# The first modulation weights and the residual rows are loaded ahead of the constants' second part and the long filters' tables

## The chip, the core and the metric

The kernel runs on one core of one Trainium2 chip. The metric is the time of one execution on the device in microseconds (us). The core's engines work side by side, each through its own instructions in order: PE (matrix multiplication), DVE (vector), ACT (scalar and table functions), POOL (general purpose) and SP (which here only issues DMA transfers). ACT and POOL issue transfers too.

## The reference, cut to what matters

The kernel computes two layers of a token trunk over 256 context tokens and 256 latent tokens (512 rows of 1024 numbers, float32). Every layer modulates and normalises the rows, projects them into three mixers (a long convolution called Hyena, a gated delta rule called GDN, and attention), merges these and goes through a mixture of experts. The change touches the first layer's start, of which this is the part:

```python
def hyena_filters(L, lp):                       # depends on weights alone, not on x
    ...
    z = jnp.concatenate([t, jnp.cos(f * w), -jnp.sin(f * w)], axis=-1)
    hdn = jnp.sin(freq * (z @ lp['hy_f_w1'] + lp['hy_f_b1']))
    hdn = jnp.sin(freq * (hdn @ lp['hy_f_w2'] + lp['hy_f_b2']))
    h = hdn @ lp['hy_f_w3']
    window = jnp.exp(-t * jnp.abs(lp['hy_decay'])) + HY_MOD_SHIFT
    return h * window                           # goes through an rfft before its use

def gdn_features(qkv, a, b, lp):
    qkv = jax.nn.silu(centred_conv(qkv, lp['gdn_conv_w']))
    ...
    g = -jnp.exp(lp['gdn_a_log']) * jax.nn.softplus(a + lp['gdn_dt_bias'])
    beta = jax.nn.sigmoid(b)

# each layer: shift, scale and gate are silu(c) @ w_ada + b_ada;
# h = rms_norm(x) * (1 + scale) + shift; then one input projection p = h @ w_in,
# whose columns are cut into hyena, q, k, v, a, b, the rotary key and the rest
```

## The kernel before, in words

The kernel is one long program that a planner writes at build time. Every instruction goes through a helper (`Lane.call`, line 210), so that all of them carry line 210 in the profile; they are told apart by their tiles. The planner keeps an estimated clock for each engine and decides from it which ready piece of work is written next. On the chip each engine then runs its list strictly in order.

The pieces are of two kinds. **Items** form the main line: each has some loads (`loads`) and work behind them (`post`). `enqueue` puts the loads of items in a queue, and `pump` issues them, each into a page (`pg`, 256 or 512 KB) of on-chip memory; `pump(force=n)` issues n of them at once. **Streams** are generators (`start`, `step`) that run beside the main line: after each `yield` the planner fits the stream's next part between items.

The first layer's start has these parts:

- `ada_items(0, 0)`: the first two of the layer's modulation vectors, as 16 tiles 128x1024 of `w_ada` (512 KB each) and two rows of `b_ada`, loaded on SP's queue. PE multiplies each tile by the condition `sc` (four matmuls 128x512 to a tile, in two loop steps of two). `ada_post` then copies the result from the accumulator (`bank`), turns it and makes `t_mod` and `t_A`, the shift and scale of each channel.
- `load_x`: four tiles of rows 128x1024 (x and ctx), loaded on ACT's queue. `norm_rows` squares and sums them on ACT and normalises them.
- `make_h`: 32 transposes on PE, and behind them eight pieces of h: scale and shift on DVE (128x256), a cast to the rounded type on ACT (the high part), and a subtraction on DVE or POOL (the low part). A product with such a pair takes three matmuls.
- `abkr`: the first projection block, for the gates a and b and the rotary key (24 matmuls 128x512). Its weights lie at tile `pg_28`. Behind it come the gates: `t_beta`, `t_gt`, `t_nal`, `t_gg`.
- `qkv(0)`: six projection blocks k0, k1, q0, q1, v0, v1 (24 matmuls each), each followed by a short convolution and silu on ACT and DVE. Eight transposes behind v1 stand at the end of this part.
- the stream `filters(0)`: the Hyena filters. Its loads (`dft` 512 KB, `hy_decay` 512 KB, `hy_f_w3` 256 KB on SP; six small ones on POOL) are issued when it is started. Then: Abs of `hy_decay`, a cast of `dft`, two Exp on ACT, two rounds of (matmul 64x256, six or seven DVE operations, Sin on ACT), four matmuls 64x512 with `w3` that give the filters, and after these 48 matmuls 128x512 with the table `dft`. The last part is held until `make_h` is written (`self.hold`, "first").
- `cst[1]`: the second part of the constants, 128x1468 (734 KB), one load on SP.
- the stream `vectors(0)` and `gains(0)`: small vectors, loaded by POOL.

What each engine does next at the start is set by three things: the order in which the loads stand on SP's queue, the planner's order of the streams' parts among the items, and on the chip the wait of each instruction for its inputs.

Of the kernel before, what the change touches and what calls it, by code (L numbers as in the profile page):

```python
# [111 lines left out]
CFIRST = COFF["ones"][0]  # L112
# [246 lines left out]
class Trunk:  # L359
# [1994 lines left out]
    def build(self):  # L2354
        nc, M, a = self.nc, self.M, self.a
# [2 lines left out]
        self.cond()  # L2358
        plan0 = self.ada_items(0, 0)
        items = self.layer(0)  # L2360
        nc.sync.dma_start(out=self.cst[1], in_=a["cst"][:, CFIRST:])
        self.start("filters", self.filters(0))
        self.gains(0)
        self.start("vectors", self.vectors(0))
        self.enqueue(plan0)
        xs = self.load_x(0)
        self.enqueue(items)
        self.pump(force=21)
        xn = []

        def norm():
# [196 lines left out]
```

## Time and profile before

| | |
|---|---|
| median of three runs | 2118.0 us (2116.41 to 2120.69) |
| the profiled execution's own time | 2112.58 us |
| its span in the trace | 2110.9 us |
| PE busy | 1853.4 us, 88% of the span |
| DVE busy | 1296.4 us, 61% |
| ACT busy | 855.6 us, 41% |
| POOL busy | 338.4 us, 16% |
| DMA moved | 402.67 MB, mean 191 GB/s |

All times of a trace count from the span's start and come from the one profiled execution. The granted clock (PEclk) is the share of full TensorE speed: 1.00 is 2.4 GHz and 0.50 is 1.2 GHz. A matmul that is written as fp32r runs on rounded operands. An idle time in brackets stands ahead of the instruction that ended it, with what that instruction waited for.

### The profile page before, as it was taken

What the parts mean: (1) busy time and instruction counts of PE and PEld (TensorE: products, weight loads), DVE (VectorE), ACT (ScalarE), POOL (GpSimd) and SP (SyncE); (2) the same over time, 40 slices, a digit from 0 to 9 for tenths busy, and PEclk for the clock granted to TensorE, in tenths of its full rate; (3) what the DMA queues carried; (4) which work ended last, traced back from release to release, by engine and by line L of the source; (5) the groups of instructions that cost most, each with busy time, mean ns of one, the idle gap of its engine ahead of it and who ended that gap; (6) DMA issues with size and microseconds to landing.
All of it is one profiled execution on the core that took longest, in us unless ns stands there. A gap on an engine that the chain in (4) does not pass through costs nothing. (4 is left out here: it accounts for less than half of the span.)

```text
span 2110.9 us, 32623 instructions
## 1 busy us (share of the span) xinstructions
PE 1853.4 (88%) x12413; PEld 1368.1 (65%) x12414; DVE 1296.4 (61%) x2775; ACT 855.6 (41%) x1477; POOL 338.4 (16%) x318
## 2 busy tenths in 40 slices
PE   5899989999999998699999289977999966899993
PEld 1776777777768776588888176966778855333330
DVE  2667666655576567899999567675777846111113
ACT  3342423344434423388887344523455421011101
POOL 1211221000123004311100211111012203100002
PEclk8999999999999999899999699988999986999996
DMA  9727111402362456699994839223324458699961
GB/s 332 249 82 214 56 40 52 124 21 81 120 180 59 120 189 248 230 373 384 378 383 177 276 137 291 67 43 94 80 80 132 132 174 333 225 394 390 383 239 69
DMA packets 295617, 402.67 MB, mean 191 GB/s; under 512 B 43941, under 2 KB 185771, under 8 KB 295449
## 3 DMA queue, kind: packets, MB, share of 16 engines
q1 hardware_dynamic: 271512, 360.38, 50.9%
q0 software_dynamic: 11040, 19.81, 2.8%
q10 hardware_dynamic: 12896, 20.28, 2.7%
q8 instruction: 100, 1.64, 0.3%
q14 instruction: 69, 0.56, 0.1%
HBM read 393.52 MB, written 23.20 MB: 197 GB/s over the span
## 5 line engine op out<-in xcount | busy, mean ns | idle before, releaser
L210 PE MATMUL bank<-pg,pg 128*128 128x512 f32 (+7 forms) x10732 | 1663.8, 390 | 77.0 <-ACT pg L210 48.0
L210 PEld LDWEIGHTS bank<-pg,pg 128*128 128x128 f32 (+5 forms) x10732 | 1212.9, 167 | 476.8 <-issue 199.2
L210 DVE TENSOR_TENSOR pg<-pg,pg 128x1024 fp32r<-128x1024 f32 (+14 forms) x697 | 603.2, 897 | 169.3 <-ACT pg L210 158.8
L210 ACT CAST pg<-pg 128x1024 fp32r<-128x1024 f32 (+3 forms) x460 | 427.9, 965 | 235.0 <-DVE pg L210 157.8
L210 ACT COPY pg<-bank 128x512 f32<-128x512 f32 (+5 forms) x414 | 171.0, 444 | 346.0 <-PE bank L210 301.7
L210 PE MATMUL bank<-cst,pg 128*128 128x128 f32 (+3 forms) x935 | 144.7, 292 | 103.8 <-DVE pg L210 49.7
L210 PEld LDWEIGHTS bank<-cst,pg 128*128 128x128 f32 (+1 forms) x935 | 117.8, 159 | 156.7 <-issue 54.1
L210 POOL TENSOR_TENSOR pg<-pg,pg 128x512 f32<-128x512 f32 (+3 forms) x77 | 131.6, 1714 | 446.2 <-DVE pg L210 274.1
L210 ACT ACTIVATE pg<-bank 128x512 f32<-128x512 f32 (+1 forms) x116 | 60.7, 534 | 197.2 <-PE bank L210 175.0
L210 DVE SCALAR_TENSOR_TENSOR pg<-bank,vec,pg 128x510 f32<-128x510 f32 (+3 forms) x112 | 73.5, 657 | 56.1 <-ACT pg L210 54.2
L210 DVE SCALAR_TENSOR_TENSOR pg<-pg,bank 128x512 f32<-128x512 f32 (+1 forms) x92 | 54.2, 601 | 84.6 <-ACT pg L210 72.3
L210 ACT ACTIVATE pg<-pg 128x512 f32<-128x512 f32 (+4 forms) x71 | 49.0, 698 | 138.7 <-DVE pg L210 123.4
L210 POOL DMA_INDIRECT yd<-pg,t_vi x28 | 29.0, 1037 | 467.6 <-ACT pg L210 232.0
L210 POOL TENSOR_TENSOR pg<-pg 128x512 f32<-128x512 f32 (+1 forms) x18 | 20.4, 1142 | 454.5 <-ACT pg L210 306.9
L210 DVE TENSOR_TENSOR pg<-bank,pg 128x512 fp32r<-128x512 f32 (+4 forms) x120 | 69.1, 596 | 30.7 <-ACT pg L210 23.5
L210 DVE COPY pg<-bank 128x512 f32<-128x512 f32 x24 | 16.6, 692 | 112.1 <-PE bank L210 90.8
L210 DVE TENSOR_TENSOR pg<-pg,bank 128x512 f32<-128x512 f32 (+1 forms) x44 | 27.0, 613 | 79.8 <-PE bank L210 77.0
L210 ACT CAST pg<-bank 128x512 fp32r<-128x512 f32 (+1 forms) x72 | 35.7, 517 | 96.9 <-PE bank L210 72.7
L210 ACT ACTIVATE pg<-bank,t_amx,t_asq 128x512 f32<-128x512 f32 (+1 forms) x48 | 33.9, 707 | 75.1 <-DVE t_amx L210 75.1
L210 ACT ACTIVATE pg<-bank,vec 128x512 f32<-128x512 f32 (+3 forms) x64 | 41.3, 646 | 53.6 <-PE bank L210 47.3
L210 PE MATMUL bank<-pg,sc 128*32 128x512 f32 x384 | 53.9, 634 | 0.7 <-DMA pg<-in_w_ada_dram 0.7
L210 DVE TENSOR_REDUCE pg<-pg 128x128 f32<-128x1024 f32 (+15 forms) x128 | 43.1, 336 | 4.4
(250 smaller groups left out, 785.0 us busy)
## 6 DMA issues: line engine op xcount, KB each, us to landing
pg<-in_moe_w_dram SPq DMA_DIRECT2D x384, 512.0 KB
pg<-in_w_in_dram SPq DMA_DIRECT2D x120, 512.0 KB
pg<-in_w_ada_dram SPq DMA_DIRECT2D x96, 512.0 KB
pg<-in_w_out_dram SPq DMA_DIRECT2D x24, 512.0 KB
pg<-modd ACTq DMA_DIRECT2D x12, 512.0 KB
pg<-yd SPq DMA_DIRECT2D x12, 512.0 KB
pg<-in_mla_w_uq_dram SPq DMA_DIRECT2D x16, 288.0 KB
pg<-gcd POOLq DMA_DIRECT2D x16, 256.0 KB, 3.8
```

The lines of the kernel that those rows point to most:

```text
L210: return f(*a, **k)
```

## The change

Two calls move behind the loads of the modulation weights, the small vectors and the rows of x: the load of `cst[1]` and the start of the stream `filters(0)`. `pump` is split: 18 loads (the 16 tiles of `w_ada` and the two rows) come first, and the three others (of the item abkr and the first block) behind. No arithmetic is added or removed.

```diff
--- before.py
+++ after.py
@@ -2358,14 +2358,15 @@
         self.cond()
         plan0 = self.ada_items(0, 0)
         items = self.layer(0)
-        nc.sync.dma_start(out=self.cst[1], in_=a["cst"][:, CFIRST:])
-        self.start("filters", self.filters(0))
         self.gains(0)
         self.start("vectors", self.vectors(0))
         self.enqueue(plan0)
         xs = self.load_x(0)
+        self.pump(force=18)
+        nc.sync.dma_start(out=self.cst[1], in_=a["cst"][:, CFIRST:])
+        self.start("filters", self.filters(0))
         self.enqueue(items)
-        self.pump(force=21)
+        self.pump(force=3)
         xn = []
 
         def norm():
```

The planner then orders the rest anew. The rows below are from the engines' instruction lists in program order; `x2` counts repeats, `<-` separates the output from the inputs, and the numbers behind a tile's name only tell tiles apart. First SP's queue, before, from its third transfer, and the end of the modulation loads:

```order
4 L210 DMA cst_72<-in_cst_dram 128x1468
5 L210 DMA pg_5_105<-in_dft_dram 128x1024
6 L210 DMA pg_4_104<-in_hy_decay_dram 128x1024
7 L210 DMA pg_3_103<-in_hy_f_w_dram 64x1024
8 L210 DMA pg_10_136<-in_w_ada_dram 128x1024
9 L210 DMA pg_11_138<-in_w_ada_dram 128x1024
...
25 L210 DMA pg_27_170<-in_w_ada_dram 128x1024
26 L210 DMA pg_28_172<-in_w_in_dram 128x8x16
```

And the same queue in the changed kernel:

```order
4 L210 DMA pg_7_120<-in_w_ada_dram 128x1024
5 L210 DMA pg_8_122<-in_w_ada_dram 128x1024
...
21 L210 DMA pg_24_154<-in_w_ada_dram 128x1024
22 L210 DMA cst_72<-in_cst_dram 128x1468
23 L210 DMA pg_27_162<-in_dft_dram 128x1024
24 L210 DMA pg_26_161<-in_hy_decay_dram 128x1024
25 L210 DMA pg_25_160<-in_hy_f_w_dram 64x1024
26 L210 DMA pg_28_172<-in_w_in_dram 128x8x16
```

The four transfers of `cst`, `dft`, `hy_decay` and `hy_f_w3` (2.06 MB) now stand between the modulation tiles and the weights of abkr, and the place of abkr in the queue is unchanged. On POOL's queue the filters' small transfers stand behind those of the vectors in the same manner.

Next ACT's list. Before, the filters' Abs, cast, two Exp and two Sin (the 64x256 rows) stand ahead of the squares of the rows of x (`t_rma`), and the cast of abkr's weights and of k0's weights (`pg_29`) stand far behind:

```order
10 L210 ACTIVATE pg_4_104<-pg_4_104 128x1024
11 L210 CAST pg_35_197<-pg_5_105 128x1024
12 L210 ACTIVATE pg_38_202<-pg_4_104,cst_72 128x1024
13 L210 ACTIVATE pg_39_204<-pg_4_104,cst_72 128x1024
14 L210 ACT_TABLE_LOAD
15 L210 ACTIVATE pg_37_201<-pg_37_201 64x256
16 L210 COPY vec_216<-bank_66 128x113
17 L210 ACTIVATE pg_37_201<-pg_37_201 64x256
18 L210 ACTIVATE pg_50_272,t_rma<-pg_6_128 128x1024
...
31 L210 CAST pg_69_357<-pg_28_172 128x1024
...
43 L210 CAST pg_88_492<-pg_29_176 128x1024
```

In the changed kernel, with what each row waits for behind it (`DVE_49` is DVE, `PE_49` is PE, `Pool_49` is POOL, `DMAHW...` a transfer; the first row is the last cast of h, and the Sin are the 64x256 rows):

```order
29 L210 CAST pg_68_376<-pg_63_339 128x512 [waits DVE_49]
30 L210 ACTIVATE pg_26_161<-pg_26_161 128x1024 [waits DMAHW5_49]
31 L210 CAST pg_70_386<-pg_27_162 128x1024 [waits DMAHW2_49]
...
34 L210 CAST pg_75_413<-pg_29_176 128x1024 [waits DMAHW1_49,PE_49]
35 L210 COPY pg_72_390<-bank_67 16x512 [waits DMAHW6_49,PE_49]
...
40 L210 ACT_TABLE_LOAD [waits DMAHW3_49,DMAHW4_49,DVE_49]
41 L210 ACTIVATE pg_2_102<-pg_2_102 64x256 [waits Pool_49]
42 L210 ACT_TABLE_LOAD
43 L210 ACTIVATE t_beta<-bank_69 128x32 [waits DVE_49]
...
47 L210 ACTIVATE pg_78_526<-pg_72_390 128x512 [waits DVE_49,Activation_49]
48 L210 ACT_TABLE_LOAD [waits DVE_49]
49 L210 ACTIVATE pg_2_102<-pg_2_102 64x256 [waits PE_49]
```

The filters' work on ACT has moved behind the casts of h. The two Sin now alternate with the gates (`t_beta`) and the short convolution of k0 (row 47). Rows 40 to 48 hold three table loads, where the kernel before had one ahead of both Sin and one ahead of `t_beta`. The loads of rows 40 and 48 carry the wait for DVE that is the wait for the argument of the Sin behind them; the one of row 42 waits for nothing.

Last PE's list. Before, the matmuls of the two sine rounds (rows 7 and 17) and the four filter matmuls (`pg_3`, the tile of `hy_f_w3`) lie among and right behind the modulation tiles (`sc`):

```order
7 L210 MATMUL bank_65<-pg_2_102,t_fw_99 64x256
...
17 L210 MATMUL bank_67<-pg_37_201,t_fw_100 64x256
...
21 L210 MATMUL bank_64<-pg_25_166,sc 32x512 x2
22 L210 MATMUL bank_68<-pg_3_103,pg_37_201 128x512
23 L210 MATMUL bank_69<-pg_3_103,pg_37_201 128x512
24 L210 MATMUL bank_64<-pg_26_168,sc 32x512 x2
...
27 L210 MATMUL bank_63<-pg_3_103,pg_37_201 128x512
28 L210 MATMUL bank_65<-pg_3_103,pg_37_201 128x512
```

In the changed kernel the same work stands behind abkr's 24 matmuls (which end at row 70): rows 71 and 89 are the sine rounds, 72 turns abkr's result, 73 to 88 are block k0, 90 works on the gates, 93 and 94 are filter matmuls, and 95 begins block k1:

```order
71 L210 MATMUL bank_68<-pg_2_102,t_fw_157 64x256
72 L210 MATMUL bank_69<-cst_71,pg_72_390 128x16 x4
73 L210 MATMUL bank_70<-pg_58_306,pg_75_413 128x512 x2
...
88 L210 MATMUL bank_70<-pg_68_376,pg_76_414 128x512
89 L210 MATMUL bank_63<-pg_2_102,t_fw_158 64x256
90 L210 MATMUL bank_65<-t_gg,cst_72 128x16 x2
...
92 L210 MATMUL bank_64<-cst_71,pg_77_423 128x113
93 L210 MATMUL bank_66<-pg_25_160,pg_2_102 128x512
94 L210 MATMUL bank_67<-pg_25_160,pg_2_102 128x512
95 L210 MATMUL bank_68<-pg_58_306,pg_81_545 128x512 x2
```

The 48 matmuls with `dft`, which stood right behind the transposes of h in the kernel before and surrounded abkr, follow in the changed kernel among the third and fourth blocks. From PE's list on behind the eight transposes after v1, both kernels have the same order.

## Rows read from the trace of the kernel before

**Rows 1.** Windows of 20 us: busy time by engine, granted clock, DMA share, GB/s.

```profile
40.00:60.00 20.00, 11.55 (x48) 8.62 (x49) 12.39 (x33) 6.98 (x11) 0.00 (x0) 0.66 1.15 323
...
80.00:100.00 20.00, 15.98 (x66) 12.63 (x65) 10.93 (x35) 7.00 (x12) 6.58 (x14) 0.91 0.81 257
...
120.00:140.00 20.00, 20.00 (x113) 15.60 (x112) 8.92 (x24) 8.52 (x14) 5.58 (x6) 1.00 0.09 27
...
160.00:180.00 20.00, 17.06 (x94) 13.48 (x93) 16.76 (x36) 4.27 (x8) 2.83 (x2) 0.91 0.63 203
```

**Rows 2.** DMA view of 35-36 us, of 37-38 us, and issues in the first 75.

```profile
DMA packets 114, 0.41 MB, mean 406 GB/s; under 512 B 15, under 2 KB 15, under 8 KB 114
...
DMA packets 1542, 0.17 MB, mean 165 GB/s; under 512 B 1540, under 2 KB 1540, under 8 KB 1542
...
cst<-in_cst_dram SPq DMA_DIRECT2D x1, 734.0 KB
```

**Rows 3.** Timeline 0-40 us: start, duration, engine, tile, count, idle time before.

```profile
10.51 1.06 ACT L210 ACTIVATE pg<-pg 128x1024 f32<-128x1024 f32 x1 [5.04 <-DMA pg<-in_hy_decay_dram]
...
12.40 2.18 ACT L210 ACTIVATE pg<-pg,cst 128x1024 f32<-128x1024 f32 x2
...
23.70 0.54 DVE L210 TENSOR_SCALAR pg<-bank,t_fv 64x256 f32<-64x256 f32 x1 [9.94 <-PE bank L210]
...
26.58 0.42 ACT L210 ACTIVATE pg<-pg 64x256 f32<-64x256 f32 x1 [10.69 <-DVE pg L210]
...
35.32 1.05 PE L210 MATMUL bank<-pg,sc 128*32 128x512 f32 x4 [0.24 <-DMA pg<-in_w_ada_dram]
...
36.30 1.98 PE L210 MATMUL bank<-pg,pg 64*128 64x512 f32 x4
```

**Rows 4.** Timeline 40-75 us.

```profile
46.69 0.58 ACT L210 COPY pg<-bank 128x512 f32<-128x512 f32 x1
...
49.45 0.38 DVE L210 SCALAR_TENSOR_TENSOR t_A<-t_mod,vec 128x4 f32<-128x4 f32 x4 [1.94 <-ACT t_mod L210]
...
55.76 1.05 ACT L210 CAST pg<-pg 128x1024 fp32r<-128x1024 f32 x1 [1.21 <-DVE pg L210]
...
56.84 1.22 DVE L210 TENSOR_TENSOR pg<-pg,pg 128x1024 fp32r<-128x1024 f32 x1 [1.16 <-ACT pg L210]
...
57.98 2.80 DVE L210 TENSOR_SCALAR pg<-bank,t_A,t_mod 128x256 f32<-128x256 f32 x6
...
60.70 0.68 DVE L210 TENSOR_TENSOR pg<-pg,pg 128x512 fp32r<-128x512 f32 x1
...
67.03 0.87 DVE L210 TENSOR_TENSOR pg<-pg,pg 128x512 fp32r<-128x512 f32 x1
```

**Rows 5.** Timeline 75-120 us.

```profile
78.02 0.57 ACT L210 COPY pg<-bank 16x512 f32<-16x512 f32 x1
...
79.46 0.87 DVE L210 TENSOR_TENSOR pg<-bank,cst 32x256 f32<-32x256 f32 x2
...
80.36 0.42 DVE L210 TENSOR_TENSOR pg<-pg,pg 32x256 f32<-32x256 f32 x1
...
86.45 1.28 ACT L210 ACT_TABLE_LOAD   x1 [4.67 <-DMA rb<-in_router_b_dram]
...
87.75 0.20 ACT L210 ACTIVATE t_beta<-bank 128x32 f32<-128x32 f32 x1
...
92.70 1.53 DVE L210 SCALAR_TENSOR_TENSOR pg<-bank,vec,pg 128x510 f32<-128x510 f32 x2
...
92.84 1.19 PE L210 MATMUL bank<-t_gg,cst 128*128 128x16 f32 x6 [3.96 <-DVE t_gg L210]
...
94.99 0.69 DVE L210 SCALAR_TENSOR_TENSOR pg<-pg,pg 128x512 f32<-128x512 f32 x1 [0.76 <-ACT pg L210]
...
100.99 16.53 PE L210 MATMUL bank<-pg,pg 128*128 128x512 f32 x70 [0.53 <-DVE pg L210]
...
117.36 1.03 PE L210 MATMUL bank<-cst,pg 128*128 128x128 f32 x8
```

## The prediction

> **What bounds the kernel now.** I read the windows first, then the timeline of the first 120 us engine by engine, then the transfers, and last the two kernels' instruction lists. Over the whole span PE is busy 88%, so PE's idle time is what can be lost or won. The windows show where it lies at the start: PE is busy 11.55 of 20 us from 40 us on, 15.98 of 20 from 80 us on, and without a gap from 120 to 140 us [rows 1]. The reader is to see two things in this. From about 118 us on PE is the bound, and what shifts its work there shifts the end. Ahead of that PE waits for ACT and DVE, and the one long wait of the blocks is 3.96 us for the gates (`t_gg`), at 88.9 us [rows 5].
>
> The landmark is the set of eight transposes behind block v1. It starts at 117.36 us [rows 5], and by then both kernels have done the same work on PE: modulation, h, abkr, six blocks, and all matmuls of the filters. Behind it PE's order is the same in both. So the forecast is the time at which the changed kernel comes to this point.
>
> **Step 1, the loads.** 734, 512, 512 and 256 KB, in sum 2.06 MB, leave the front of SP's queue. With large packets the queue moves 406 GB/s [rows 2], so the modulation tiles come 2.06 / 0.406 = 5.1 us earlier. Before, PE takes a tile at 35.32 us, two more follow at 1.29 us each (524 KB / 406 GB/s), so the last comes at 37.9 and now at 32.8; its matmuls take 1.05 us [rows 3] and end at 33.9. From the copy of the result (46.69) to the end of `t_A` (49.45 + 0.38) it takes 3.14 us [rows 4]: `t_A` stands at 37.0 and not at 49.8. That is 12.8 us won. The bounds are the full 5.1 us, and nothing if the rows of x share the rate for longer. What stands behind the four transfers, abkr's weights first, keeps its place and lands when it did (about 39.6, an estimate: at 37 to 38 us its small packets still come at 165 GB/s [rows 2]). Moving the small transfers on POOL's queue costs nothing: the filters now need them some 30 us later.
>
> **Step 2, what ACT and DVE do behind it.** Each runs in order, and the filters' work, which before lay in the time in which both waited for loads (10 to 36 us), now stands behind h. I add it up along both lists.
>
> - h starts at 37.0. Its first six DVE operations take 2.80 us and a low part 0.68 [rows 4]: about 40.4. Then DVE reorders abkr's weights (0.49, an estimate for four copies from the gap ahead of the cast): 40.9; ACT casts them, 1.05, and DVE subtracts, 1.22 [rows 4]: 43.2.
> - The rest of h: all of h takes DVE from 57.98 to 67.90 us [rows 4], 9.92, less the 3.48 done: 6.4, so 49.6.
> - The filters' Abs, cast and two Exp on ACT took from 10.51 to 14.58 [rows 3], 4.07: 53.7. The cast of k0's weights, 1.05: 54.8. The copy of abkr's result, 0.57: 55.4. On DVE k0's low part ends at 56.0, the rotary key takes 0.87 + 0.42 [rows 5], `t_tokv` an estimated 0.3: 57.6.
> - The first sine's argument takes DVE from 23.70 to 26.54 [rows 3], 2.84: 60.5. Its table load carries the wait for that argument: 1.28 [rows 5], then Sin, 0.42 [rows 3]: 62.2. The table load for the gates, 1.28: 63.5.
> - The gates, from `t_beta` at 87.75 to `t_gg`, ready when PE's wait ends at 92.84 (less 0.06): 5.03: 68.5. The convolution of k0 on DVE and its silu on ACT, from 92.70 to 95.68, 2.98 [rows 5]: 71.5.
> - The second sine's argument, 2.84: 74.3; its table load, which waits for it, and Sin, 1.70: 76.0.
>
> Only at 76.0 can PE start the four filter matmuls and block k1, which stands behind them in its list. Before, half of them ran at 36.3 us [rows 3]. In the meantime PE has only abkr and k0, some 11 us of work, and stands idle for most of 63 to 76 us. This is the new wait that takes the place of those for the modulation and the gates.
>
> **Step 3, from there to the landmark.** PE has the four filter matmuls (1.98 us for half of them [rows 3], 3.96), and of the 144 + 24 + 48 = 216 matmuls of blocks, abkr and filters all but the 48 of abkr and k0. 70 take 16.53 us [rows 5], so 168 take 39.7: 76.0 + 3.96 + 39.7 = 119.7. To that comes the clock. After the 3.96 us wait the window of 80 to 100 us has a mean grant of 0.91, 1.8 us less of full speed in 20; the window of 40 to 60 us, behind a longer idle time, has 0.66, and by PE's busy share of it (11.55 / 20) 3.9 us [rows 1]. I take 2.5, nearer the first, since from 76 us on PE has work without a gap: 122.2 us, against 117.36. The sum is **+4.8 us**.
>
> The bounds of the terms: the three table loads cost between nothing (if all run ahead of their operands) and 3.84, and I take 3.84 because two of them carry the wait; the loads' gain between 5.1 and nothing; the clock between 1.8 and 3.9. ACT also issues three small transfers ahead of the first sine. In the kernel before, ACT's table load waited 4.67 us behind the same three [rows 5]; here they stand behind loads that are long in by 57 us, so I take nothing, and at worst it is 57.3 + 4.67 - 60.5 = 1.5. That makes +1.0 to +12.0 with everything at one end, and +1.5 to +8 for what can fall together.
>
> On the table loads the trace gives 86.45 + 1.28 = 87.73 and the next ACTIVATE at 87.75 [rows 5]: 1.30 us from the load's start to the instruction behind it. The Trainium skill, "ScalarE: Activation LUTs", section "What ACT_TABLE_LOAD costs", says that a change of table costs about 1.28 us of load and 1.38 us of drain. This row shows the load and no drain. By the page the three loads would cost 3 x 1.38 = 4.1 us more, and the sum would be +8.9.
>
> **The rivals.**
>
> *The chain costs PE less, and the kernel is faster.* For it: `t_A` is 12.8 us earlier, and my sum lets ACT and DVE alternate. If they overlap, DVE alone sets the end: 9.9 of h, 0.5, three low parts (3.7), 1.7 of key and constants, 2 x 2.84, some 4.6 of gates and 2.2 of convolution are 28.3 us from 37.0, 65.3, and with the last table load and Sin 67.0. Then 67.0 + 43.7 + 1.8 = 112.5, 4.9 us faster: 2113. Against it: the lists show operands that go from one engine to the other at nearly every step. It decides if the second Sin ends before 71.2 (117.36 - 43.66 - 2.5).
>
> *A later wait takes it back.* For it: from 160 to 180 us PE is busy 17.06 of 20 us [rows 1]. If that wait ends with a load that does not move, 2.9 of the 4.8 us are lost in it: +1.9, 2120. Against it: PE is full for 40 us ahead of it, and ACT and DVE take their work from PE there.
>
> *The loads give less, or the table loads cost more.* If the rows of x on ACT's queue hold the rate, the modulation comes when it did, and the chain starts 5.1 us later: +9.9, 2128. If each of the three table loads holds ACT for twice its 1.28 us, it is 3.84 more: +8.6, 2127. The page named above speaks for this second half, since its drain is of that size. For the first half: the queue runs at its 406 GB/s already [rows 2]. Against it: x was in this stretch before as well, and the row at 86.45 has no second 1.28 us behind it [rows 5].
>
> **How the numbers follow.** The profiled execution took 2112.58 us, its span 2110.9, and the runs have a median of 2118.0: the profiled one is 5.4 below it, and I put the difference on the median. 2118.0 + 4.8 = 2122.8, about 2123. 0.2%, about what a measurement of this kernel can tell from no change, is 4.2 us. The likeliest case has 0.56, with a range of 2119.5 to 2126; its middle lies just over the bound, so I count 0.31 of it as slower and 0.25 as within 0.2%. The faster rival has 0.16, of which 0.02 within the bound. The later wait has 0.13, all within. Fewer gains or dearer tables have 0.15, all slower. In sum 0.14 faster, 0.40 same, 0.46 slower. The range goes from 2113 (the faster rival) to 2128 (the loads give nothing).
>
> **What would show it.** Right: the last modulation tile at about 33 us and `t_A` at about 37; the 24 matmuls of k0 done by 63; PE waiting on ACT for a Sin until about 76; table loads at 60, 62 and 75; a half clock behind it; the eight transposes at about 122; and the same order and gap sizes later. Wrong: `t_A` later than 40 (step 1), the second Sin ahead of 71 (step 2), PE busy through 63 to 76, or a shift at 118 us that is gone at 200.

## The result, and the profile after

The changed kernel takes 2142.2 us (median of three runs; a fourth, disturbed one of 2410 us is left out), the kernel before 2119.35 us beside it on the same chip: a ratio of 1.0106, with a 95% interval from 1.0081 to 1.0131. It is slower by about 23 us (2142.23 - 2119.35 = 22.9). The forecast was 2123 us, slower by about 5 us, with a range that ended at 2128: the sign was right, the size was not, and the result lies outside the range.

The profiled execution of the changed kernel took 2144.4 us, its span 2142.8. The profile of before that the prediction used came from an execution of 2112.58 us, 5.4 below the median, so a second trace of the same kernel before was taken (2118.81 us, span 2117.1), and shifts are counted against that one unless the text says otherwise.

First TensorE's own rows, in the timeline of the changed kernel (start, duration, engine, tile, count, and in brackets the idle time before and what ended it):

```profile
32.45 1.05 PE L210 MATMUL bank<-pg,sc 128*32 128x512 f32 x4 [0.20 <-DMA pg<-in_w_ada_dram]
...
58.85 7.35 PE L210 MATMUL bank<-pg,pg 128*128 128x512 f32 x24
...
71.80 1.49 PE L210 MATMUL bank<-t_gg,cst 128*128 128x16 f32 x6 [5.03 <-DVE t_gg L210]
76.67 0.42 PE L210 MATMUL bank<-cst,pg 113*128 113x113 f32 x1 [3.38 <-DMA t_dtb<-in_gdn_dt_bias_dram]
79.24 1.22 PE L210 MATMUL bank<-pg,pg 64*128 64x512 f32 x1 [2.15 <-ACT pg L210]
...
125.71 1.04 PE L210 MATMUL bank<-cst,pg 128*128 128x128 f32 x8
126.50 8.63 PE L210 MATMUL bank<-pg,pg 128*128 128x512 f32 x36
138.71 5.38 PE L210 MATMUL bank<-cst,pg 128*128 128x1 f32 x24 [3.58 <-ACT pg L210]
...
143.74 6.25 PE L210 MATMUL bank<-pg,pg 128*128 128x512 f32 x18
...
158.70 5.86 PE L210 MATMUL bank<-pg,pg 128*128 128x512 f32 x24
```

The same places in the second trace of the kernel before:

```profile
118.37 1.04 PE L210 MATMUL bank<-cst,pg 128*128 128x128 f32 x8
119.17 11.24 PE L210 MATMUL bank<-pg,pg 128*128 128x512 f32 x48
130.24 2.77 PE L210 MATMUL bank<-cst,pg 128*128 128x1 f32 x24
132.77 4.37 PE L210 MATMUL bank<-pg,pg 128*128 128x512 f32 x18
...
143.41 1.88 PE L210 MATMUL bank<-pg,pg 128*128 128x512 f32 x7
```

Read the two from top to bottom. The modulation's matmuls are done at 33.5 us. Behind the transposes of h, abkr and k0, PE waits for the gates, for a small vector and for a Sin, until 79.24. The eight transposes, the prediction's landmark, come at 125.71: 7.3 us late (8.35 against the first trace, 117.36 [rows 5]). Only 33 us later the shift has doubled: the block that starts at 143.41 before starts at 158.70, 15.3 us late, by which time both have done the same work. Between the two stand a new wait of 3.58 us, and 24 tiny and 18 ordinary matmuls that take 5.38 and 6.25 us instead of 2.77 and 4.37.

Far behind, the last uses of `t_gg` (second layer) stand in the tile view of the second trace before and of the changed kernel (count; min/median/max ns; first and last start in us):

```profile
L210 PE MATMUL bank<-t_gg,cst x12: 262/328/401, 93.0 to 1232.4; 128*128 128x16 f32 x8, 128*128 128x32 f32 x4
```

```profile
L210 PE MATMUL bank<-t_gg,cst x12: 201/325/401, 71.8 to 1256.9; 128*128 128x16 f32 x8, 128*128 128x32 f32 x4
```

So the shift between these two traces is 7.3 us at the landmark, 15.3 at 158 us, 24.5 at 1257, and 25.7 at the end (2142.8 - 2117.1; the medians differ by 22.9). The first number is what the prediction was about. The second is a separate event.

### The profile page after: what moved, and what is told of

It is laid out like the page before. It is cut to its first block, busy times and chain, and to the rows that moved or that the text cites. A ratio compares the mean times of both kernels' runs of the same rounds, so it can differ in the third digit from the quotient of the medians.

```text
span 2142.8 us, 32626 instructions
## 1 busy us (share of the span) xinstructions
PE 1882.5 (88%) x12413; PEld 1382.7 (65%) x12414; DVE 1300.8 (61%) x2775; ACT 858.5 (40%) x1479; POOL 335.5 (16%) x318
## 5 line engine op out<-in xcount | busy, mean ns | idle before, releaser
L210 PE MATMUL bank<-pg,pg 128*128 128x512 f32 (+5 forms) x10734 | 1687.6, 393 | 81.6 <-ACT pg L210 52.8
L210 PEld LDWEIGHTS bank<-pg,pg 128*128 128x128 f32 (+3 forms) x10734 | 1224.2, 168 | 494.3 <-issue 204.1
L210 DVE TENSOR_TENSOR pg<-pg,pg 128x1024 fp32r<-128x1024 f32 (+12 forms) x696 | 605.6, 902 | 170.9 <-ACT pg L210 163.5
L210 ACT COPY pg<-bank 128x512 f32<-128x512 f32 (+4 forms) x414 | 171.1, 444 | 349.1 <-PE bank L210 312.8
L210 DVE COPY pg<-bank 128x512 f32<-128x512 f32 x24 | 16.6, 692 | 111.4 <-PE bank L210 96.6
L210 ACT ACTIVATE pg<-bank,t_amx,t_asq 128x512 f32<-128x512 f32 (+1 forms) x48 | 33.9, 707 | 75.0 <-DVE t_amx L210 75.0
```

The source lines that it names most:

```text
L210: return f(*a, **k)
```

## The experiments

### The writes of `kd`: what happens behind the landmark

ACT's timeline in the changed kernel, at the place in question (ACTq is ACT's issuing of transfers):

```profile
114.34 0.63 ACT L210 ACTIVATE pg<-pg 128x512 f32<-128x512 f32 x1 [1.66 <-DVE pg L210]
114.39 0.98 ACTq L210 DMA_DIRECT2D kd<-pg  x2
114.88 0.56 ACT L210 COPY pg<-bank 128x512 f32<-128x512 f32 x1
116.86 3.53 ACTq L210 DMA_DIRECT2D kd<-pg  x4
120.43 1.05 ACT L210 CAST pg<-pg 128x1024 fp32r<-128x1024 f32 x1 [4.98 <-DMA kd<-pg]
126.11 0.69 ACT L210 ACTIVATE pg<-bank,vec 128x512 f32<-128x512 f32 x1 [4.63 <-DMA kd<-pg]
```

The finished filters are written out to `kd` by six transfers on ACT's queue. ACT does no work for 4.98 us, of which the issuing of the last four takes 3.53. Then a silu waits 4.63 us more: the page that it is to write is one from which a `kd` transfer still reads. It is the fifth silu of the six blocks, that of v0. The silu of v1, the sums of squares and the 24 tiny matmuls stand behind it. In the kernel before, the same six writes were issued from 71.99 to 77.02 us.

Theory: these two holds cost the second 8 us. Rival: they lie beside PE's work, and the loss is that of the Sin alone. Four kernels test this. The expectations that speak of 14 and 11 us given back count from a loss of 24.0 us, 1.1 more than the 22.9 used here.

**e1**, the six writes on POOL's queue, otherwise the changed kernel:

```diff
-                nc.scalar.dma_start(out=self.kd[l][:, :, o:o + 128].rearrange("c p x -> p c x"), in_=blk.f().rearrange("p (c x) -> p c x", c=4))
+                (nc.gpsimd if l == 0 else nc.scalar).dma_start(out=self.kd[l][:, :, o:o + 128].rearrange("c p x -> p c x"), in_=blk.f().rearrange("p (c x) -> p c x", c=4))
```

> The changed kernel, with the six writes of the filters' tables (kd, first layer) issued by POOL and not by ACT; all other instructions stand as in the changed kernel. Theory: the loss has two parts. 8.35 us are lost by the landmark (PE waits for the second Sin until 79.2 us), and about 8 more between 117 and 145 us, because ACT is held 4.98 us by the issue of these writes at 115 to 120 us and 4.63 us more at 121.5 to 126.1 by a page that such a write still reads, so that PE waits 3.58 us at 135.1 to 138.7 and then runs at half clock. Without ACT's hold that wait goes: 6 to 8 us back, about 2135 beside 2142. Rival: the second part follows from the first (the chain is late anyway, whoever issues): no change, 2142. Second rival: the pages are held by the slower writes of POOL instead, and the 4.63 us stay or grow: 2138 to 2144.

Measured: 2136.2 us, ratio 1.0081 (1.0061 to 1.0101), 18.3 us slower than its runs of before (the interval overlaps that of the changed kernel). In its ACT timeline the issuing is gone and the wait for the page is what remains, longer than before:

```profile
114.93 1.05 ACT L210 CAST pg<-pg 128x1024 fp32r<-128x1024 f32 x1
124.22 0.69 ACT L210 ACTIVATE pg<-bank,vec 128x512 f32<-128x512 f32 x1 [8.23 <-DMA kd<-pg]
```

PE's wait falls from 3.58 to 2.09 us, no more. The time is near the theory's, but the trace is that of the second rival: the page wait grew. So the pages matter, not the queue alone.

**e9**, the writes on ACT as they were, but their pages are given back some 12 us later by the planner's clock, so that v0's silu gets another page. Up to 300 us the instruction order on PE, ACT and DVE is that of the changed kernel.

```diff
+        if l == 0:
+            yield self.plan.clk["tensor"] + 12000.0
         for blk in (*kr, *ks, kz, k2):
             blk.free()
```

> The changed kernel with the kd pages given back later and the writes left on ACT. Theory: of ACT's two holds (4.98 us of issue, 4.63 us of page wait) the second goes; the normalisation behind v1 comes some 4 us earlier, PE's 3.58 us wait at 138.7 us shrinks or goes, and with it part of the half clock: 2132 to 2138. Rival (the issue alone makes ACT late): 2140 to 2143, as the changed kernel.

Measured: 2131.3 us, ratio 1.0056 (1.0034 to 1.0077). Each against its own runs of before, it is 13.0 us slower than before and the changed kernel 22.9, so 9.9 us come back. (The trace is of its fastest execution, 2123.77 us.) ACT still spends its time on issuing, but the silu follows at once, and PE does not wait. So the issuing alone does not make PE's wait:

```profile
120.28 1.05 ACT L210 CAST pg<-pg 128x1024 fp32r<-128x1024 f32 x1 [4.87 <-DMA kd<-pg]
121.23 0.68 ACT L210 ACTIVATE pg<-bank,vec 128x512 f32<-128x512 f32 x1
```

```profile
125.66 1.03 PE L210 MATMUL bank<-cst,pg 128*128 128x128 f32 x8
126.45 8.63 PE L210 MATMUL bank<-pg,pg 128*128 128x512 f32 x36
134.91 2.77 PE L210 MATMUL bank<-cst,pg 128*128 128x1 f32 x24
```

**e8**, both edits together.

> The changed kernel with the kd writes on POOL, and the pages from which they are written are given back some 12 us later in the build, so that no convolution is written into a page that a kd write still reads; the order on every engine is that of the kernel with the writes on POOL. Theory: there ACT still waited 8.23 us for such a page at 116 to 124.2 us. Without it ACT's convolutions come in time, PE's wait at 134.7 to 136.8 and the half clock behind it go, and only the 8 us of the landmark stay: 2126 to 2131. Rival (the page wait only hides a later one, or the loss behind the landmark comes from elsewhere): 2134 to 2138.

Measured: 2128.1 us, ratio 1.0045 (1.0030 to 1.0060): 9.8 us slower than before and not 22.9, so 13.1 us come back. Its landmark is at 126.31, no earlier, but the block of 158.70 starts at 151.25, 7.4 us sooner. The windows show why the loss was larger than the wait (columns as in [rows 1]: PE, PEld, DVE, ACT, POOL, granted clock, DMA share, GB/s). The changed kernel:

```profile
70.00:80.00 10.00, 2.67 (x8) 2.04 (x9) 6.16 (x18) 3.14 (x4) 2.66 (x6) 0.50 0.60 204
80.00:90.00 10.00, 10.00 (x26) 5.62 (x25) 7.52 (x16) 5.74 (x12) 0.00 (x0) 0.69 0.02 3
...
130.00:140.00 10.00, 6.42 (x29) 5.08 (x28) 4.72 (x7) 4.19 (x8) 2.08 (x2) 0.87 0.13 52
140.00:150.00 10.00, 10.00 (x39) 8.68 (x40) 4.84 (x17) 2.39 (x5) 3.49 (x4) 0.61 0.13 39
```

and e8:

```profile
130.00:140.00 10.00, 10.00 (x57) 8.60 (x56) 5.13 (x17) 4.13 (x7) 2.08 (x2) 1.00 0.14 39
140.00:150.00 10.00, 10.00 (x61) 7.34 (x63) 2.76 (x8) 4.04 (x10) 3.47 (x4) 1.00 0.67 225
```

Behind the 3.58 us wait the granted clock is 0.61 in the mean of 140 to 150 us, for most of it the lower of the two levels, 1.2 GHz; in e8, without the wait, it is 1.00. The sum from landmark to the 158 us block: 3.58 of wait, 2.61 on the tiny matmuls (5.38 - 2.77), 1.88 on the 18 (6.25 - 4.37), 8.07 against the measured 8.0 (15.3 - 7.3).

**b3**, the pages kept in the kernel before, where the writes lie at 72 us.

> The second half of the control: the kernel before with the kd pages given back later and the writes left on ACT. In the changed kernel this edit alone took 11 us. In the kernel before no instruction on PE's path waits for a kd write's page up to the landmark. Theory: nothing, 2114 to 2121; then the 11 us are the price of a page conflict that only the change makes. Rival (the pages cost the kernel before the same): 2105 to 2110.

Measured: 2119.9 us, ratio 1.0008 (0.9992 to 1.0023): nothing. So what e9 gives back belongs to the changed kernel alone: the change carried the writes from a place where nobody on PE's path waits for their pages to one where v0 does. With the pages kept in both, the change costs 11.6 us (13.0 - 1.4) and not 22.9. For the pages the rival is out. For the queue it is not: see b1 below.

### What holds PE until 79 us

PE's rows name three waits in turn, and each could be the one that counts.

**t1**, Tanh in place of the first layer's two Sin (the filters get other numbers), so that the table loads of ACT fall away; further lines, not shown, keep the planner's order.

```diff
...
-            nc.scalar.activation(hh, x, AF.Sin)
...
+            nc.scalar.activation(hh, x, AF.Sin if l else AF.Tanh)
...
```

> The changed kernel with the first layer's two Sin replaced by Tanh, so that four table loads go (the three on the path of the second sine and the one behind it) and nothing else moves on any engine; the first layer's Hyena filters are then other numbers. Theory: the three loads stand open on the path, 1.28 us each, so the second activation ends about 3.8 us earlier (75.4 and not 79.2 us), the landmark comes 3 to 4 us earlier (122), and the writes and their waits behind it stay: 2136 to 2140. Rival (the loads are hidden behind the sines' arguments on DVE): landmark at 125 to 126, 2142.

Measured: 2135.6 us, ratio 1.0083 (1.0067 to 1.0098), landmark 124.31. The landmark gains only 1.4 us, since another wait stood right beside the Sin, that of one PE instruction which turns the second layer's small vectors:

```profile
76.92 0.42 PE L210 MATMUL bank<-cst,pg 113*128 113x113 f32 x1 [6.85 <-DMA t_nal<-in_gdn_a_log_dram]
```

**u1** starts the stream of these vectors behind block v1, **u2** does that and takes Tanh as well.

```diff
-        self.start("vectors", self.vectors(1))
-        self.gains(1)
...
+        if l == 0:
+            items += [hook(lambda: (self.start("vectors", self.vectors(1)), self.gains(1)))]
```

> The changed kernel with the small vectors of the second layer (nine transfers on POOL, and the transposes 113x113 on PE) started behind block v1; nothing else moves up to the landmark. In the changed kernel these transposes stand ahead of the filter matmuls, and PE waited 3.38 us for the transfers, until 76.67 us, and then 2.15 us more for the second Sin, until 79.24. Theory (the Sin sets the end): PE waits longer for Sin instead, landmark 125 to 126, time 2138 to 2143. Rival (the transfers set it): landmark 122 to 123, 2136 to 2139.

> The same with Tanh in place of the first layer's two Sin, so that the table loads go as well (the filters are then other numbers). With the table loads alone away, the landmark came only 1.4 us earlier (124.31), and PE waited 6.85 us for the transfers of the second layer's vectors. Theory (Sin and transfers stood side by side, and either hides the other): with both away the landmark comes 3 to 4.5 us earlier than in the changed kernel, 121.2 to 122.7. Rival (another wait stands right behind, as DVE's chain through the gates): 124 or more.

Measured: u1 2134.75 us (1.0082, 1.0062 to 1.0102), u2 2132.5 us (1.0065, 1.0045 to 1.0084). PE's rows at the start of the four filter matmuls, of u1 and of u2:

```profile
79.56 6.63 PE L210 MATMUL bank<-pg,pg 64*128 64x512 f32 x10 [6.02 <-ACT pg L210]
```

```profile
75.37 6.63 PE L210 MATMUL bank<-pg,pg 64*128 64x512 f32 x10 [5.38 <-ACT pg L210]
```

With the vectors away PE starts no earlier (79.56 against 79.24), and without the table loads it starts 4.19 us earlier, the landmark at 122.51 and not 126.53. So the chain to the second Sin sets the place, as the prediction had it, and the vectors stood hidden beside it. u1's time was missed: it is 17.2 us slower than its runs of before, where the changed kernel is 22.9 slower, though its landmark is 0.8 us later. Its trace shows where most of this lies. The late vectors moved other work too: the `kd` writes are issued from 110.04 us and not from 114.39, no silu's wait is put down to their pages (a cast's is, 2.21 us), and ahead of the 24 tiny matmuls stand 42 matmuls instead of 36. PE's wait there falls from 3.58 to 1.52 us, with no slow matmuls behind it:

```profile
138.79 2.88 PE L210 MATMUL bank<-cst,pg 128*128 128x1 f32 x24 [1.52 <-ACT pg L210]
```

The block that starts at 158.70 in the changed kernel starts at 153.94 in u1, 4.8 us earlier.

### The change in parts

**c1**, only `cst[1]` goes behind the modulation, and the filters' loads stay ahead.

> One part of the change alone: the load of the constants' second part is moved behind the 18 loads, the filters' start stays in front. The filters' Exp need these constants, and they stand on ACT ahead of the squares of x. Theory: Abs and the cast run early, the first Exp waits until the constants are in at about 37 us, the squares and with them the modulation's copy and h come no earlier than before (copy at 46 to 49), and the second Sin follows h: 2128 to 2140. Rival (this part is harmless, the whole loss comes from the filters' tables): 2116 to 2122.

Measured: 2130.6 us, ratio 1.0052 (1.0033 to 1.0071), landmark 133.77. The two Exp take their scale from `cst[1]` and stand on ACT ahead of the squares of x; ACT waits 27.52 us for that load, until 39.25, and PE 12.38 us for the modulation's copy. This part alone loses 12 us by a mechanism that the full change does not have. (The trace is of its slowest execution, 2141.35 us.)

**e3**, the loads as before, and the filters' computation held until h, so that the lists read as in the changed kernel.

> The kernel before with its loads as they were, but the first layer's filter stream is held until h is written, so that ACT, DVE and PE have nearly the lists of the changed kernel. Theory: the order alone costs the time; the modulation comes 5 us later than in the changed kernel, so that the chain behind it starts 5 us later too: 2145 to 2150. Rival (the later loads of hy_decay, dft and the constants cost the time, not the order): 2117 to 2122, as before. Second rival (the start of the modulation does not matter to the chain): 2142, as the changed kernel.

Measured: 2138.7 us, ratio 1.0086 (1.0068 to 1.0105), landmark 129.14. The order alone costs 20.8 us (2138.7 - 2117.9), and the modulation that comes 5 us earlier brings the landmark 3.4 us forward (129.14 - 125.71). At the end none of this is left: e3 is not slower than the changed kernel (20.8 against 22.9 us, with intervals that overlap), and my 2145 to 2150 was missed. The second event comes with the order as well. ACT's two holds are there with 5.05 and 4.86 us, and so is PE's wait:

```profile
142.53 5.38 PE L210 MATMUL bank<-cst,pg 128*128 128x1 f32 x24 [4.05 <-ACT pg L210]
```

What the change was to win is small beside what the order costs.

**e2**, the changed kernel with the sine rounds (`rounds`, whose lines are not shown) ahead of Abs, the cast and Exp; **e6**, that and the `kd` writes on POOL.

```diff
...
+        if l == 0:
+            yield max(self.plan.when(x) for x in (zt.f(256), w1, w2, fv))
+            hdk += [M.get(), M.get()]
+            yield from rounds(zt.f(256)[:33])
         yield max(self.plan.when(x) for x in (dec.f(), dft.f(), zt.f(256), self.cst[1]))
...
```

> The changed kernel's loads, but the first layer's filter stream does its two sine rounds first, as soon as the small tables are in (they need neither hy_decay nor dft), and Abs, cast and Exp behind them. Theory (order on ACT and DVE behind h is the cause): the two Sin run while the modulation tiles still come, the four filter matmuls come behind the transposes, PE no longer waits for Sin at 66 to 79 us; the modulation still comes 5 us earlier. Abs, cast and two Exp stay ahead of h's casts (4 to 5 us). Landmark 113 to 118 us, time 2112 to 2120. Rival (the place of the loads in the queue is the cause, the filters' big tables come too late): 2135 or more.

> The two edits together: the changed kernel with the sine rounds first and the kd writes on POOL. Theory: as the kernel with the sine rounds first, and up to 3 us less, since the kd writes then stand where ACT has little on PE's path: 2109 to 2120. Rival: POOL's writes delay what reads the pages or kd: 2120 to 2130.

Measured: e2 2132.3 us (1.0056, 1.0034 to 1.0078), landmark 121.67; e6 2125.55 us (1.0036, 1.0026 to 1.0046), landmark 120.84. My expectations of a kernel about as fast as before failed (e2 is 14.4 us slower, e6 7.6): the second Sin now stands on ACT ahead of the squares of x, which start behind it at 31.79, and PE waits 7.93 us at the modulation's copy, until 41.28. One wait was traded for another, though for a shorter one.

**n2**, the kernel before with its normalisation two items into the modulation instead of six, so that h comes earlier without any move of loads.

```diff
-        plan0.insert(6, Item(post=lambda it: norm()))
+        plan0.insert(2, Item(post=lambda it: norm()))
```

> The kernel before with one number changed: the normalisation of the rows is written behind the second item of the modulation and not behind the sixth, so that on ACT the squares of the rows of x stand ahead of the second Sin, and not behind it. All loads stand as before. Theory: in the kernel before the squares waited until 35.2 us behind that Sin and the modulation's copy until 46.69, though its last matmul was done by 39.3; with the squares ahead, the copy runs at 40 to 41, h comes 4 to 6 us earlier, and the filters stay where they are: 2112 to 2116. Rival (the second sine round, now behind the squares, comes later and takes it back): 2117 to 2121.

Measured: 2120.6 us, ratio 1.0009 (0.9996 to 1.0023). `t_A` comes 7.6 us earlier than in the kernel before, the landmark 1.0 to 2.1 us (116.31, against 117.36 and 118.37 in the two traces). My theory that an early h is worth its time is wrong: DVE takes 12.4 us for the pieces of h (49.48 to 61.88) where it took 9.9 before, so that h ends 6.0 us earlier, and at 81 us PE waits 3.35 us ahead of the transpose of the second layer's vectors.

### Versions that could beat both

**b1** is the kernel before with both `kd` edits; **b2** adds n2's edit; **u4** adds to b1 the late vectors; **s1** has the changed kernel's loads, the sine rounds during the loads, the normalisation one item in, and both `kd` edits; **u3** is s1 with the late vectors; **r1** is the kernel before, once more.

> The control: the kernel before with the kd writes on POOL and their pages given back later, which took 14 us from the changed kernel. In the kernel before ACT's holds by these writes (4.51 us at 72.5 to 77 and 4.67 us at 81.8 to 86.45) come where PE has filter matmuls and blocks, and only the 3.96 us wait for the gates and some half clock hang on them. Theory: 2 to 6 us faster, 2112 to 2116, so that most of the 14 us belongs to the place into which the change moves the writes. Rival (the writes cost the same everywhere): 2104 to 2108. Second rival: nothing, 2118.

> The kernel before with the normalisation earlier, the kd writes on POOL and their pages given back later. With the normalisation alone the landmark came 1 us earlier; ACT was held 7.42 us by the issue of the kd writes at 79.4 to 86.85, and PE waited 3.35 us at 81 to 84.3. Theory: this wait goes, 3 to 6 us faster than before: 2112 to 2116. Rival: DVE's work behind h bounds PE whatever ACT does: 2117 to 2121.

> A version that may beat both: the kernel before with the kd writes on POOL, their pages given back later, and the second layer's small vectors behind block v1. The first two edits alone gave 2107.7 us; in their trace PE waited 2.49 us for these vectors' transfers at 93.4 to 95.9 us. Theory: that wait goes: 2103 to 2108. Rival: POOL's writes delay the vectors into the work behind the landmark: 2108 to 2114.

> A version that may beat both: the changed kernel's loads; on ACT the squares of x first, then the two sine rounds while the modulation tiles come, then h, and only Abs, cast and two Exp of the filters behind h; kd writes on POOL, pages given back later. Theory: the modulation's copy at 34 us as in the changed kernel, h from 36 us, no wait for Sin and one table load on ACT behind h; the filter matmuls wait for no more than h itself. The chain of the changed kernel from the cast of the filters (54 us) to PE's start on full work loses its two sine arguments, two table loads and two Sin, and PE is fed from about 62 us on: landmark 107 to 114, time 2106 to 2114. Rival (DVE's work behind h bounds PE): landmark 116 to 119, 2117 to 2121.

> A version that may beat both: the changed kernel's loads, the squares of x first, the sine rounds during the loads, only Abs, cast and two Exp of the filters behind h, kd writes on POOL with pages given back later, and now the second layer's small vectors behind block v1. Without the last edit it took 2109.8 us, with the landmark at 119.87 us and PE waiting 5.26 us for those vectors' transfers up to 77.8 us. Theory: the wait goes and PE goes on with the filter matmuls at about 72.6 us: landmark 113.5 to 116, time 2103 to 2109. Rival (DVE's chain sets the end there too): landmark 118 to 120, 2108 to 2112.

> The kernel before, unchanged, for a second trace of it. The first trace came from an execution of 2112.58 us, some 6 us below the median of its runs. If that difference lies behind the first layer's mixers, in work that the change does not touch, the landmark is again at 117.2 to 117.6 us and the two traces agree to 1 us up to 700 us; if it lies in the start, the landmark is later by some us and the loss of the changed kernel there is smaller than 8.35 us.

| kernel | median us | ratio to before (95%) | landmark us |
|---|---|---|---|
| b1 | 2107.7 | 0.9950 (0.9935 to 0.9965) | 114.01 |
| b2 | 2121.4 | 1.0016 (1.0006 to 1.0026) | 112.30 |
| u4 | 2113.1 | 0.9975 (0.9964 to 0.9986) | 111.45 |
| s1 | 2109.8 | 0.9954 (0.9940 to 0.9968) | 119.87 |
| u3 | 2126.8 | 1.0040 (1.0023 to 1.0056) | 123.71 |
| r1 | 2118.35 | 1.0006 (0.9993 to 1.0019) | 118.37 |

b1 is faster than the kernel before by 0.5%, and s1 is with the changed kernel's loads. Most of the expectations failed. b1 and u4 came out where their rivals stood, b2 just above its rival, and u3 above every range. s1's time lies in its range, but its landmark is far behind the 107 to 114 of its theory: that was luck.

b1 limits what e8 showed. I had forecast that the two `kd` edits would give the kernel before 2 to 6 us, and they give it 11.5, nearly the 13.1 of the changed kernel. The kept pages alone give it nothing (b3), so the queue matters there: with ACT free of the writes, PE waits 0.85 us for the gates and not 3.96 [rows 5]. Against b1, e8 is still 21.3 us slower (9.8 + 11.5). So the page conflict is a price of the change (e9 and b3), while the issuing of the writes from ACT costs the kernel before as well.

The landmark does not foretell the end across kernels whose later order differs: b2 has an early landmark and no gain, s1 a late one and a gain. b1's gain of 11.5 us (2119.14 - 2107.66) is only in part at the landmark (4.4 against the second trace). Where the rest comes from was not settled. Why u3's landmark is 3.8 us behind that of s1 its trace shows: DVE waits 7.48 us for `t_iob` on POOL, POOL 14.98 us for a small load that ACT issues at 62.23 us behind others, and the gates are late: PE waits 10.01 us for `t_gg`. The rest of the 17 us between the two was not settled.

## Why the prediction was wrong in size, point by point

**Step 1, the loads: right.** The last modulation matmuls end at 33.50 (forecast 33.9). From here on DVE's timeline of the changed kernel:

```profile
36.01 0.39 DVE L210 SCALAR_TENSOR_TENSOR t_A<-t_mod,vec 128x4 f32<-128x4 f32 x4 [6.03 <-ACT t_mod L210]
36.31 1.90 DVE L210 TENSOR_SCALAR pg<-bank,t_A,t_mod 128x256 f32<-128x256 f32 x4
39.78 0.99 DVE L210 TENSOR_SCALAR pg<-bank,t_A,t_mod 128x256 f32<-128x256 f32 x2 [1.57 <-DMA modd<-pg]
40.69 0.68 DVE L210 TENSOR_TENSOR pg<-pg,pg 128x512 fp32r<-128x512 f32 x1
...
45.90 1.74 DVE L210 TENSOR_TENSOR pg<-pg,pg 128x512 fp32r<-128x512 f32 x1
...
49.56 1.74 DVE L210 TENSOR_TENSOR pg<-pg,pg 128x512 fp32r<-128x512 f32 x1
...
52.32 0.68 DVE L210 TENSOR_TENSOR pg<-pg,pg 128x512 fp32r<-128x512 f32 x1
...
63.44 0.28 DVE L210 TENSOR_SCALAR pg<-pg 64x256 f32<-64x256 f32 x1
...
71.56 0.19 DVE L210 TENSOR_TENSOR t_gg<-t_gt,t_nal 128x32 f32<-128x32 f32 x1
...
77.11 0.28 DVE L210 TENSOR_SCALAR pg<-pg 64x256 f32<-64x256 f32 x1
```

`t_A` ends at 36.40 (forecast 37.0).

**Step 2, the chain: the mechanism right, h mis-sized by 4 us.** The term was "The rest of h: ... so 49.6". From `t_A` to the end of h it took 52.32 + 0.68 - 36.40 = 16.6 us and not 12.6. Two things make 3.7 us of it: a wait of 1.57 us for a page that the write of `modd` still reads, and two low parts of 1.74 us instead of 0.68 (2.12 in sum). With `t_A` 0.6 us early, h ends 3.4 us late, and this is nearly all of the landmark's 3.5 us beyond the forecast (125.71 - 122.2). Everything behind h was sized right: 26.4 us were forecast from there to the end of the second Sin, and 26.2 were taken. ACT's rows:

```profile
63.79 1.28 ACT L210 ACT_TABLE_LOAD   x1 [3.28 <-DMA rw<-in_router_w_dram]
65.08 0.42 ACT L210 ACTIVATE pg<-pg 64x256 f32<-64x256 f32 x1
65.52 1.28 ACT L210 ACT_TABLE_LOAD   x1
...
77.48 1.28 ACT L210 ACT_TABLE_LOAD   x1 [3.56 <-DVE pg L210]
78.77 0.42 ACT L210 ACTIVATE pg<-pg 64x256 f32<-64x256 f32 x1
```

The reader is to see that two of the three loads start only when DVE's argument is done (63.44 + 0.28, 77.11 + 0.28), so that each lies on the path with its 1.28 us. The first row names a transfer (`rw`), but the argument ends 0.07 us ahead of the load, so it is the likelier releaser. The loads cost 4.2 us at the start of the filter matmuls and 4.0 at the landmark (u1 against u2), near the 3.84 that the sum took for three. The drain of the Trainium skill ("ScalarE: Activation LUTs", "What ACT_TABLE_LOAD costs"), 4.1 us more for three, is not in these rows: the next ACTIVATE starts 0.01 to 0.02 us behind each load. By the page's figures u2 would have gained about 7.9 us (an estimate), and it gained 4.2.

**Step 3, to the landmark: right.** 46.2 us were forecast from the Sin to the transposes, 46.5 measured (125.71 - 79.19). The clock behind the wait is in it: 0.69 in 80 to 90 us.

**What failed: "From about 118 us on PE is the bound, and what shifts its work there shifts the end", and "the same order and gap sizes later".** With e9 the sentence holds as far as the 158 us block: the shift is 7.3 us at the landmark and 7.2 there (150.58 - 143.41), and with e8 it is 7.9 and 7.8. In the changed kernel as it is, the `kd` writes, which the change moves with the filters and which the step's list left out, hold ACT and a page just where v0 needs them. That made the second 8 us, and the kept pages bring 9.9 us of the median back. I followed the moved stream's inputs and its work, up to its last matmul, but not what it puts out.

My statement that PE's list is the same from the eight transposes on was not exact either. Before, 48 matmuls stand between them and the 24 tiny ones, in the changed kernel 36: 12 of them come behind. At 16.53 / 70 us apiece [rows 5] that is 2.8 us less of cover for the late normalisation. With this cover the wait would have been some 0.8 us. This is argued and was not tried alone; u1, with 42, has 1.52 us, but there the writes come earlier too.

**The rivals.** The faster rival needed the second Sin ahead of 71.2; it ended at 79.19. The later wait that takes the shift back did not come: the shift grew. None of the rivals had a wait behind the landmark that makes the shift grow. The loads gave what they should, and the table loads cost what the sum took.

**What stays open.** From 158 us on the shift grows from 15.3 to 25.7 us in small steps, in nearly the same order of instructions. Without the `kd` holds (e8) it grows from 7.8 to 9.6 in the traces. But t1, which has both holds (4.88 and 4.37 us), grows from 12.4 to 14.4 only, and e3 from 19.0 to 22.4. And the two traces of the unchanged kernel before, 1.0 us apart at the landmark, are 6.2 apart at the end (2117.1 - 2110.9). So the growth is not shown to go with the holds, part of it can be the difference between single executions, and what makes the rest was not found.

## What to carry to other kernels

A stream that is moved takes its outputs along: list the transfers that it issues last, the engine that issues them, and who gets the pages that they read, beside its inputs and its work. An early start of one chain is worth what the next engine's pace allows (5 us earlier here gave 3.4 at the landmark, 7.6 us gave 1 to 2), while the work that was moved onto the lists behind that start added up link by link (26.2 us, 26.4 summed). Try an edit that mends the changed kernel on the kernel before as well: here the kept pages gained in the changed kernel alone, and the writes' move to POOL in both. Where a forecast rests on a landmark, check the lists for some tens of instructions behind it, and the waits there that have little cover.

## What the runs showed of the hardware that was not expected

**DVE and POOL in each other's way, with either as the loser.** The low parts of h are the same instruction on both engines. Alone, DVE takes 0.68 us (the row at 52.32) and POOL 1.29. Side by side, in POOL's timeline of the kernel before and then of the changed one:

```profile
60.62 1.92 POOL L210 TENSOR_TENSOR pg<-pg,pg 128x512 fp32r<-128x512 f32 x1 [44.85 <-ACT pg L210]
```

```profile
45.80 1.28 POOL L210 TENSOR_TENSOR pg<-pg,pg 128x512 fp32r<-128x512 f32 x1 [5.60 <-ACT pg L210]
49.47 1.28 POOL L210 TENSOR_TENSOR pg<-pg,pg 128x512 fp32r<-128x512 f32 x1 [2.38 <-ACT pg L210]
```

Before, POOL's operation beside DVE's at 60.70 (0.68) [rows 4] is the longer one, by 0.63 us; in the changed kernel DVE's at 45.90 and 49.56 are, by 1.06. In both, one engine has the time that it takes alone, and the other has nearly the sum. The Trainium skill, "SBUF — State Buffer", section "SBUF: two separate sides", says that the two engines share a port pair as an exclusive lock, which whichever starts first holds for its whole instruction. The sums agree with a lock. That the first one wins does not show in these records: POOL starts 0.08 us ahead of DVE before and 0.10 us ahead after, with opposite losers; POOL's spans are rough, so this stays unsettled. For a forecast it means that a duration of such a pair, taken from one timeline, can turn by 1 us for each pair from one kernel to another.

**A short wait with a long tail.** PE's 3.58 us of idle time at 135 us was followed by a mean grant of 0.61 in 140 to 150 us, which cost 4.5 us more than the wait itself (2.61 + 1.88); e9 and e8, which do not have that wait, run the same 24 tiny matmuls in 2.77 us.
